# Emitting the four query tiles of the input projection inside the preparation of the recurrent heads, with a z buffer of their own

## The chip, the cores and the metric

The kernel runs on one core of a Trainium2 chip. The metric is the device time of one execution in microseconds (us). A core has five engines that run side by side, each with its own queue of instructions: TensorE (PE in the profile, matrix products), VectorE (DVE), ScalarE (ACT), GpSimd (POOL) and SyncE (SP, which only issues transfers here). An engine takes its queue in order, and an instruction starts when what it depends on is there.

## The reference, cut to what matters

One step of a decoder layer with two kinds of heads, for 512 prompt rows and 8 x 4 sample rows. Everything is fp32.

```python
xp = ffn_half(xp, ffn1_norm, ffn1_wg, ffn1_wu, ffn1_wd)         # the same for the sample rows xs
zp = rms_norm(xp, mix_norm) @ w_in                              # one projection, columns split among the heads
qp, kvp, gp = nsa_heads(zp[..., :NSA_COLS])                     # 512 query, 6 x 128 key/value, 24 gate columns
o_nsa = nsa_prompt(qp, kvp, gp, cmp_w, rel_bias_table)          # compressed, selected and window attention
o_rw, wkv, shift = rwkv_mix(zp[..., NSA_COLS:], ...)            # RWKV-7: token shift, decay, delta rule
xp = xp + concat([o_nsa, o_rw]) @ w_out
xp = ffn_half(xp, ffn2_norm, ffn2_wg, ffn2_wu, ffn2_wd)
y  = rms_norm(xp, final_norm)
```

In `nsa_prompt` the compressed branch takes a softmax of queries times block summaries of the keys (at most 8 blocks); the summed probabilities also choose the blocks of the selected branch.

## The kernel before, in words

The stages follow one another: first feed-forward half, input projection with recurrent heads and attention, output projection, second half. Activations lie as columns, 128 features by 2 x 272 rows (16 sample rows and 256 prompt rows in each half, `SW` to `HW`). A large product is split into a high and a low part of each operand and summed from three products, so one column tile of the input projection (`win_tile`, L385, 8 blocks of the contraction) is 48 matmuls of 128x128 by 128x272 on L155, and its weights are loaded by SyncE (`wraw`, L144) and split by ScalarE (`wh`, L146) and VectorE (`wl`, L148).

There are 25 column tiles. `rwkv_prep` (L511) takes tiles 0 to 13 for the recurrent heads: it loops over two pairs of heads per call and is called twice (head pairs 0 and 1, then 2 and 3). Per pair it forms rates, decays and normalised keys on ScalarE and VectorE (L545 to L574) and multiplies them into blocks (L581). `rwkv_inverse` (L615) inverts the block triangles with a ladder of 30 dependent VectorE instructions between two transposes (L619 to L641). `rwkv_chain` (L681) runs the recurrence, `rwkv_sample` (L761) the sample rows.

`nsa_in` (L407) takes tiles 14 to 24, one for i = 0 to 10: i = 0 to 3 are the queries, 4 and 5 the keys and values for compression, 6 and 8 keys (selected, window), 7 and 9 their values, 10 the gates. It multiplies the sums by the norm `r` into a tile `z`, and stores that to memory through ScalarE's queue (`zq` for queries, `out_kv` for the rest). Values are transposed on TensorE (L434) into `vr`; keys are split into `kk` by four ScalarE copies (L445) and four VectorE differences (L446); i = 8 also writes `out_owk`. The order of the eleven is `ZORD = (0, 1, 2, 3, 4, 5, 10, 7, 9, 6, 8)`.

Queries are read back from `zq`: by `prompt_cmp` as `zr`, four loads of one query tile each through two buffers (L1256), for the scores of the compressed branch (L1258), their softmax (L1259 to L1273), a transpose (L1276) and its copy `PcmT` (L1277); and by the attention as `qd`.

Tiles come from pools. A pool's tag has a fixed number of buffers used in turn: `z` has the tag `xr` of the pool `rot`, two buffers, which the block operands `bk` of the preparation and all z tiles share. PSUM holds two sums of dense tiles (`acc`). The order on each engine is not that of the code: a scheduler reorders instructions when the kernel is built, mostly by the order in which the code emits them and by when their inputs and buffers are thought ready. On the chip each engine then runs its queue strictly in that order. Cache gathers (`kv`, L997) and small loads (`gsum`, L1017) stand in SyncE's queue; the tags of some `kv` buffers are those of the projection's activations (`hh`, `hl`), so they are free when the last dense matmul has read these.

Of the kernel before, what the change touches and what calls it, by code (L numbers as in the profile page):

```python
# [7 lines left out]
F32 = mybir.dt.float32  # L8
# [15 lines left out]
ZORD = (0, 1, 2, 3, 4, 5, 10, 7, 9, 6, 8)  # L24
# [3 lines left out]
HW = 272  # L28
# [19 lines left out]
class Step:  # L48
# [44 lines left out]
    def v(self, i):  # L93
        return self.vec[:, i:i + 1]
# [243 lines left out]
    def mix(self):  # L338
        nc = self.nc
        r = self.norm_end()  # L340
        with ExitStack() as st:
            self.mc = self.pool("mc", 1, st)
            self.un = self.pool("un", 1, st)
            self.orw = self.mc.tile([128, 4, 2, HW], F32, name="orw")
            un1 = self.un1 = self.pool("u1", 1, st)
            with ExitStack() as s0:
                un0 = self.pool("u0", 1, s0, side="right")
                with ExitStack() as s2:
                    self.rwkv_setup(s2)
                    self.lanes = "p"  # L350
                    S0 = self.rwkv_prep(0, r, un0)
                    self.lanes = "q"
                    self.rwkv_inverse(S0[0])
                    self.lanes = "p"
                    S1 = self.rwkv_prep(1, r, un1)
                    nc.scalar.dma_start(self.O["sh"], self.sho.rearrange("p a b -> p (a b)"))
                self.lanes = "q"
                self.ch = self.pool("ch", 1, s0, side="right")
                self.rwkv_chain(0, un0, *S0)
                self.rwkv_inverse(S1[0])  # L360
            self.az = self.pool("az", 1, st, side="right")
            with ExitStack() as s3:
                self.lanes = "p"
                yo = self.rwkv_sample(self.pool("rs", 1, s3, side="right"))
                self.lanes = "q"
                self.ch = self.pool("ch1", 1, s3, side="right")
                self.rwkv_chain(1, un1, *S1)
            self.rwkv_sample_out(yo)
            self.un1 = un1
            self.lanes = "p"  # L370
            self.at = self.pool("at", 1, st, side="right")
            for i in ZORD[0:4]:
                self.nsa_in(i, r)
            self.nsa_open()
            for i in ZORD[4:7]:
                self.nsa_in(i, r)
            cmp = self.prompt_cmp(*self.prompt_blocks())
            for i in ZORD[7:]:
                self.nsa_in(i, r)
            self.attention_setup()  # L380
            bias = self.prompt_bias()
            self.attention(bias, cmp)
            self.w_out()
# [23 lines left out]
    def nsa_in(self, i, r):  # L407
        nc, O = self.nc, self.O
        p = self.win_tile(14 + i)
        if i == 10:  # L410
            nc.vector.tensor_mul(self.gT[:24], p[:24, :, :HW], r[:24])
            nc.scalar.activation(self.gT[:24], self.gT[:24], AF.Sigmoid)
            return
        z = self.rot.tile([128, 2, HW], F32, name="z", tag="xr")
        zt = z[:, :, SW:HW]
        if i < 4:
            nc.vector.scalar_tensor_tensor(z, p[:, :, :HW], 0.125, r, op0=OP.mult, op1=OP.mult)
            nc.scalar.dma_start(self.zq[:, i], z)
            return
        nc.vector.tensor_mul(z, p[:, :, :HW], r)  # L420
        nc.scalar.dma_start(O["kv"][i - 4], z)
        if i < 6:
            for g in range(2):
                for ch in range(2):
                    nc.scalar.activation(self.px[ch * 64:ch * 64 + 64, i - 4, g],
                                         zt[g * 64:g * 64 + 64].rearrange("p h (b c j) -> p h b c j", b=4, c=2)[:, :, :, ch], AF.Copy)
            return
        nc.gpsimd.tensor_copy(self.new[:, i - 6].rearrange("p (h t) -> p h t", h=2), z[:, :, 0:SW])
        b = i // 2 - 3
        if i % 2:  # L430
            p = self.ps()
            for j in range(4):
                c0 = SW + (j % 2) * 128
                nc.tensor.transpose(p[:, j * 128:j * 128 + 128], z[:, j // 2, c0:c0 + 128], self.ident)  # L434
            nc.scalar.activation(self.vr[:, b], p.rearrange("p (j g d) -> p j g d", j=4, g=2), AF.Copy)
            return
        if i == 8:
            for h in range(2):
                nc.scalar.dma_start(O["owk"][4 * h:4 * h + 4, :, 508:512].rearrange("n p t -> p n t"),
                                    z[:, h, 0:SW].rearrange("p (n t) -> p n t", t=4))  # L440
        v = lambda x: x.rearrange("p (h t) -> p h t", h=2)
        for g in range(2):
            for x in range(2):
                zg, k2 = zt[g * 64:g * 64 + 64], self.kk[b][x * 64:x * 64 + 64, g]
                nc.scalar.activation(v(k2[:, 0]), zg, AF.Copy)  # L445
                nc.vector.tensor_sub(v(k2[:, 1]), zg, v(k2[:, 0]).bitcast(F32))  # L446
# [64 lines left out]
    def rwkv_prep(self, si, r, up):  # L511
# [20 lines left out]
        for pi in range(2):  # L532
            p = 2 * si + pi
# [76 lines left out]
            nc.vector.tensor_mul(self.gbs[:, 1, p], samp(pb[0]), samp(v))  # L610
            nc.vector.tensor_mul(c64(self.orw[:, p, 0, SW:HW]), half(pb[0][:, ZS:ZP[0][1]]), half(v[:, ZS:ZP[0][1]]))
            nc.vector.tensor_mul(c64(self.orw[:, p, 1, SW:HW]), half(pb[1][:, :ZW - ZP[1][0]]), half(v[:, ZP[1][0]:ZW]))
        return L, BK, UV, ar, pcp

    def rwkv_inverse(self, L):  # L615
# [979 lines left out]
```

## Time and profile before

| | before |
|---|---|
| time, three runs, us | 1405.24, 1395.78, 1404.97 |
| median, us | 1404.97 |
| profiled execution: time / span, us | 1392.31 / 1390.5 |
| mean granted TensorE clock | 0.974 |
| TensorE busy | 1315.2 us, 95% |
| VectorE, ScalarE, GpSimd busy | 51%, 37%, 19% |
| mixing stage up to the last projection tile | about 500 to 784 us |
| attention | about 784 to 928 us |

The profile is of one execution. Its times are microseconds from the first instruction. A row names an engine, a source line, an operation, out<-in by the program's tile names, partitions and shape; PE is TensorE's multiplying and PEld its loading of weights. [...] An idle time in brackets stands just ahead of the instruction, with what ended it; a transfer's row on a queue is the time of its issue, not of its flight.

### The profile page before, as it was taken

How to read it: one execution, taken by the hardware profiler on the slowest of the kernel's cores; microseconds unless marked ns; L12 is line 12 of the kernel's file. 1: busy time of each engine (PE TensorE's matmuls, PEld its weight loads, DVE VectorE, ACT ScalarE, POOL GpSimd, SP SyncE). 2: the span in 40 equal slices, each digit the busy share in tenths (PEclk: the TensorE clock that was granted, in tenths of full speed). 3: DMA queues.
4: the chain of work that ended last, by engine and by line, in shares of the span. 5: the costliest groups of instructions: out<-in, count | busy, mean ns of one | idle time of the engine just before them, and what ended most of it. 6: DMA issues, size and time to landing. Idle time of an engine off the chain costs nothing.

```text
span 1390.5 us, 31672 instructions
## 1 busy us (share of the span) xinstructions
PE 1315.2 (95%) x13313; PEld 1240.6 (89%) x13313; DVE 706.4 (51%) x1357; ACT 512.7 (37%) x925; POOL 258.9 (19%) x317
## 2 busy tenths in 40 slices
PE   6999999999999998998999779989999999999996
PEld 6999999999999977787678667769999999999996
DVE  6443343333333558869685675765544444442224
ACT  5232232233222555451223455754433333332231
POOL 2073567530000111210003214301000000000000
PEclk9999999999999999699999889999999999999998
DMA  4464465544443311112225528625322222233332
GB/s 157 162 197 121 149 201 186 174 132 116 124 118 114 112 54 46 34 41 73 73 78 180 149 72 243 201 79 179 100 92 84 91 86 90 88 100 108 102 105 84
DMA packets 99328, 163.25 MB, mean 117 GB/s; under 512 B 16185, under 2 KB 42881, under 8 KB 98546
## 3 DMA queue, kind: packets, MB, share of 16 engines
q1 hardware_dynamic: 74258, 114.71, 26.8%
q0 software_dynamic: 9040, 25.24, 6.1%
q10 hardware_dynamic: 15888, 21.28, 5.0%
q8 instruction: 105, 1.72, 0.5%
q14 instruction: 37, 0.30, 0.1%
HBM read 150.19 MB, written 16.72 MB: 120 GB/s over the span
## 4 chain that ended last, share of the span: by engine, by line
PE 68%; DVE 6%; ACT 3%; DMA 3%; issue 2%; POOL 0%; SPq 0%; ACTq 0%; DVEq 0%; POOLq 0%
PE acc L155 53%; PE pp L949 1%; PE pq L952 1%; PE po L949 1%; PE pS L949 1%; DMA kv<-in_slc 1%; PE pq L697 1%; PE pp L480 1%; PE pp L581 1%; DMA kv<-in_slc,idx 1%; DVE ivt L636 1%; PE pq L155 1%; PE pq L722 1%; PE pp L859 0%; DMA kv<-in_wkv 0%
## 5 line engine op out<-in xcount | busy, mean ns | idle before, releaser
L155 PE MATMUL acc<-hl,wh 128*128 128x272 f32 x2064 | 427.4, 292 | 3.9 <-ACT wh L146 3.9
L146 ACT ACTIVATE wh<-wraw 128x512 fp32r<-128x512 f32 x338 | 209.7, 621 | 581.9 <-PE acc L155 537.2
L155 PE MATMUL acc<-hh,wh 128*128 128x272 f32 x1808 | 384.1, 293 | 9.1 <-ACT hh L104 9.1
L148 DVE TENSOR_TENSOR wl<-wraw,wh 128x512 fp32r<-128x512 f32 x338 | 232.0, 687 | 306.2 <-ACT wh L146 304.3
L155 PE MATMUL acc<-hh,wl 128*128 128x272 f32 x1808 | 381.3, 292 | 1.6 <-DVE wl L148 1.6
L155 PEld LDWEIGHTS acc<-hl,wh 128*128 128x128 f32 x2064 | 325.3, 191 | 9.4 <-ACT wh L146 4.2
L155 PEld LDWEIGHTS acc<-hh,wh 128*128 128x128 f32 x1808 | 288.1, 190 | 14.5 <-ACT hh L104 9.1
L155 PEld LDWEIGHTS acc<-hh,wl 128*128 128x128 f32 x1808 | 285.5, 190 | 4.4 <-DVE wl L148 1.9
L903 POOL DMA_INDIRECT cp<-in_cmp,idx x128 | 131.1, 1024 | 98.6 <-issue 37.2
L122 POOL TENSOR_TENSOR ss<-ss,sq 128x544 f32<-128x544 f32 x23 | 31.6, 1374 | 612.4 <-ACT sq L118 597.0
L155 PE MATMUL acc<-ah,wh 128*128 128x272 f32 x660 | 136.9, 289 | 0.0
L155 PE MATMUL acc<-al,wh 128*128 128x272 f32 x660 | 136.3, 288 | 0.0
L155 PE MATMUL acc<-ah,wl 128*128 128x272 f32 x660 | 135.6, 286 | 0.0
L155 PEld LDWEIGHTS acc<-al,wh 128*128 128x128 f32 x660 | 104.0, 188 | 0.0
L155 PEld LDWEIGHTS acc<-ah,wl 128*128 128x128 f32 x660 | 103.3, 188 | 0.0
L155 PEld LDWEIGHTS acc<-ah,wh 128*128 128x128 f32 x660 | 103.0, 188 | 0.0
L190 DVE TENSOR_TENSOR u<-acc,r 128x544 f32<-128x544 f32 x42 | 30.4, 724 | 74.8 <-PE acc L155 74.8
L188 DVE TENSOR_TENSOR t<-acc,r 128x544 f32<-128x544 f32 x42 | 30.4, 724 | 74.1 <-PE acc L155 74.1
L903 POOL DMA_INDIRECT kv<-in_slc,idx x48 | 47.1, 982 | 108.8 <-DVE Y L730 60.3
L193 ACT ACTIVATE ah<-u 128x544 fp32r<-128x544 f32 x44 | 29.0, 658 | 64.1 <-DVE u L191 64.1
L194 DVE TENSOR_TENSOR al<-u,ah 128x544 fp32r<-128x544 f32 x44 | 31.9, 724 | 29.0 <-ACT ah L193 29.0
L1352 ACT ACTIVATE Sp<-Sp,st 128x512 f32<-128x512 f32 (+3 forms) x64 | 35.4, 554 | 9.1 <-DVE st L1350 7.4
(495 smaller groups left out, 1438.8 us busy)
## 6 DMA issues: line engine op xcount, KB each, us to landing
wraw<-in_wg SPq DMA_DIRECT2D x88, 256.0 KB
wraw<-in_wu SPq DMA_DIRECT2D x88, 256.0 KB
wraw<-in_wd SPq DMA_DIRECT2D x80, 256.0 KB
wraw<-in_win SPq DMA_DIRECT2D x50, 256.0 KB
kv<-in_slc SPq DMA_DIRECT2D x80, 128.0 KB
x<-xr ACTq DMA_DIRECT2D x16, 272.0 KB
xr<-x ACTq DMA_DIRECT2D x16, 272.0 KB
kv<-in_wkv SPq DMA_DIRECT2D x8, 512.0 KB
```

What stands on the lines that cost most here:

```text
L122: nc.gpsimd.tensor_add(self.ss, self.ss, sq)
L146: nc.scalar.activation(wh[:, :m], w[:, :m], AF.Copy)
L148: nc.vector.tensor_sub(wl[:, :m], w[:, :m], wh[:, :m].bitcast(F32))
L155: self.nc.tensor.matmul(p[h] if isinstance(p, list) else p[:, h, :HW], a, b[:, h], start=f, stop=l)
L188: nc.vector.tensor_mul(t, pt, r)
L190: nc.vector.tensor_mul(u, pu, r)
L193: nc.scalar.activation(ah[:, f], u, AF.Copy)
L194: nc.vector.tensor_sub(al[:, f], u, ah[:, f].bitcast(F32))
L480: self.nc.tensor.matmul(p[h][:, :b - a], lhsT, rhs[:, a:b], start=True, stop=True)
L903: self.nc.gpsimd.indirect_dma_start(out=tile[:, k], out_offset=None, in_=rows, in_offset=bass.IndirectOffsetOnAxis(ap=self.idx[:, k0 + k:k ...
L949: self.tc.keep_in_program_order(self.nc.tensor.matmul(*args, **kw))
L1352: nc.scalar.activation(S[g][:, :N], S[g][:, :N], AF.Exp, bias=st[:, g:g + 1], scale=-1.0, accum_out=st[:, 2 + g:3 + g])
```

## The change

The four query tiles are no longer emitted ahead of `nsa_open`; each pair of heads in `rwkv_prep` emits one of them at the end of its loop. Their `z` gets a tile `zz` from the pool of the preparation, one buffer, freed with that pool. Lines from L374 to L610 of before are two less after, those from L611 on one less.

```diff
--- before.py
+++ after.py
@@ -369,8 +369,6 @@
             self.un1 = un1
             self.lanes = "p"
             self.at = self.pool("at", 1, st, side="right")
-            for i in ZORD[0:4]:
-                self.nsa_in(i, r)
             self.nsa_open()
             for i in ZORD[4:7]:
                 self.nsa_in(i, r)
@@ -411,7 +409,7 @@
             nc.vector.tensor_mul(self.gT[:24], p[:24, :, :HW], r[:24])
             nc.scalar.activation(self.gT[:24], self.gT[:24], AF.Sigmoid)
             return
-        z = self.rot.tile([128, 2, HW], F32, name="z", tag="xr")
+        z = self.tp.tile([128, 2, HW], F32, name="zz") if i < 4 else self.rot.tile([128, 2, HW], F32, name="z", tag="xr")
         zt = z[:, :, SW:HW]
         if i < 4:
             nc.vector.scalar_tensor_tensor(z, p[:, :, :HW], 0.125, r, op0=OP.mult, op1=OP.mult)
@@ -610,6 +608,7 @@
             nc.vector.tensor_mul(self.gbs[:, 1, p], samp(pb[0]), samp(v))
             nc.vector.tensor_mul(c64(self.orw[:, p, 0, SW:HW]), half(pb[0][:, ZS:ZP[0][1]]), half(v[:, ZS:ZP[0][1]]))
             nc.vector.tensor_mul(c64(self.orw[:, p, 1, SW:HW]), half(pb[1][:, :ZW - ZP[1][0]]), half(v[:, ZP[1][0]:ZW]))
+            self.nsa_in(p, r)
         return L, BK, UV, ar, pcp
 
     def rwkv_inverse(self, L):
```

What the scheduler makes of it is shown at three places.

VectorE, in the preparation of head pair 2, around the end of the ladder of the first inverse (`ivt`, `ivN`). Before:

```order
L637 TENSOR_REDUCE ivN<-ivt 128x2x14
L557 SCALAR_TENSOR_TENSOR sig<-xs_k,vec,sig 128x560
L636 TENSOR_TENSOR ivt<-ivN,ivA 128x450
L560 TENSOR_TENSOR xs_k<-xs_k,sq_6205 128x560
L637 TENSOR_REDUCE ivN<-ivt 128x2x15
L561 TENSOR_TENSOR a<-sig,a 128x560
L639 STREAM_TRANSPOSE ivDt<-ivN 128x32x32
L641 STREAM_TRANSPOSE ivDn<-ivN 128x32x32
L570 TENSOR_TENSOR bk_6447<-a,sq_6205 128x512
L571 TENSOR_TENSOR bk_6448<-xs_k,sq_6205 128x512
```

After:

```order
L638 STREAM_TRANSPOSE ivDt<-ivN 128x32x32
L640 STREAM_TRANSPOSE ivDn<-ivN 128x32x32
L551 TENSOR_SCALAR sig<-pp 128x300
L551 TENSOR_SCALAR sig<-pp 128x260
L148 TENSOR_TENSOR wl<-wraw,wh 128x512
L659 TENSOR_TENSOR ivDt<-pq,ivDt 32x16x16 x2
L555 SCALAR_TENSOR_TENSOR sig<-xs_k,vec,sig 128x560
L558 TENSOR_TENSOR xs_k<-xs_k,sq_6333 128x560
L559 TENSOR_TENSOR a<-sig,a 128x560
L415 SCALAR_TENSOR_TENSOR zz<-acc,r 128x544
L568 TENSOR_TENSOR bk_6575<-a,sq_6333 128x512
L569 TENSOR_TENSOR bk_6576<-xs_k,sq_6333 128x512
```

The products that form `sig`, `xs_k` and `a` of pair 2 stood inside the ladder and ahead of its transposes; they now stand behind both transposes, and the query product `zz` stands between them and the block operands `bk`.

TensorE, at the end of the projection: dense matmuls (L155, `acc`), scores of the compressed branch, transposes of its probabilities (`Pm`) and of the values (`z`). Lines of "..." leave out dense matmuls only. Before, with 20 dense matmuls left out behind the second row, then 6, 51, 6 and 64:

```order
L1258 MATMUL pp<-kcd,zr 128x16 x8
L480 MATMUL pq<-sg,g_5019 128x260
...
L1258 MATMUL pp<-kcd,zr 128x16 x4
...
L1258 MATMUL pp<-kcd,zr 128x16 x4
...
L1276 MATMUL pp<-ident,Pm 64x128 x4
L434 MATMUL pp<-ident,z 128x128 x4
...
L434 MATMUL pp<-ident,z 128x128 x4
...
L883 MATMUL pp<-hid,w_8816 128x512
```

After, with 3 left out and then 13:

```order
L1257 MATMUL pp<-kcd,zr 128x16 x8
...
L1236 MATMUL pp<-w_8816,hx 64x64
...
L1257 MATMUL pp<-kcd,zr 128x16 x8
L1275 MATMUL pp<-ident,Pm 64x128 x4
L432 MATMUL pp<-ident,z 128x128 x8
L882 MATMUL pp<-hid,w_8816 128x512
```

The second half of the scores and all the transposes now stand behind the last dense matmul of the projection.

VectorE at the same place: the end of the softmax (`Pm`, `cmx`), the copy `PcmT`, query splits (`qs`) and the products `z` of the tiles i = 6 and 8. Before:

```order
L1273 TENSOR_TENSOR Pm<-Pm,cmx 128x256
L148 TENSOR_TENSOR wl<-wraw,wh 128x512 x2
L1277 COPY PcmT<-pp 64x512
L420 TENSOR_TENSOR z<-acc,r 128x544
L1329 SCALAR_TENSOR_TENSOR qs<-qd,qs 64x512
L446 TENSOR_TENSOR kk<-z,kk 64x512 x4
L1329 SCALAR_TENSOR_TENSOR qs<-qd,qs 64x512
L420 TENSOR_TENSOR z<-acc,r 128x544
L886 COPY kccT<-pp 64x256 x2
```

After:

```order
L1272 TENSOR_TENSOR Pm<-Pm,cmx 128x256
L1276 COPY PcmT<-pp 64x512
L1328 SCALAR_TENSOR_TENSOR qs<-qd,qs 64x512
L418 TENSOR_TENSOR z<-acc,r 128x544 x2
L1328 SCALAR_TENSOR_TENSOR qs<-qd,qs 64x512
L885 COPY kccT<-pp 64x256
L444 TENSOR_TENSOR kk<-z,kk 64x512 x4
L885 COPY kccT<-pp 64x256
```

In both orders the products stand behind the copy; the two are now next to each other, and no weight split stands between them and the softmax.

## Rows read from the trace of the kernel before

**Rows 1.** Page: the span, and TensorE's busy time, share and instructions.

```profile
span 1390.5 us, 31672 instructions
PE 1315.2 (95%) x13313; PEld 1240.6 (89%) x13313; DVE 706.4 (51%) x1357; ACT 512.7 (37%) x925; POOL 258.9 (19%) x317
```

**Rows 2.** Stretches: length; busy PE, PEld, DVE, ACT, POOL; granted clock; DMA share; GB/s.

```profile
500.00:784.00 284.00, 263.99 (x4156) 223.15 (x4155) 204.29 (x381) 106.64 (x180) 40.32 (x83) 0.96 0.24 76
500.00:540.00 40.00, 34.57 (x400) 30.60 (x400) 25.94 (x47) 20.72 (x35) 9.62 (x25) 1.00 0.14 45
540.00:571.00 31.00, 28.41 (x262) 24.46 (x254) 29.80 (x57) 16.09 (x25) 2.94 (x14) 0.89 0.14 47
571.00:599.00 28.00, 25.91 (x671) 23.01 (x673) 16.40 (x28) 10.36 (x20) 7.72 (x13) 0.70 0.11 34
599.00:629.00 30.00, 26.46 (x394) 22.69 (x393) 22.03 (x34) 15.53 (x24) 4.04 (x10) 1.00 0.14 46
```

**Rows 3.** Timeline, TensorE, preparation: start, length, what [idle before <-releaser].

```profile
536.13 1.10 PE L581 MATMUL pp<-ar,bk 64*64 64x128 f32 x32 [1.91 <-DVE ar L574]
...
556.04 1.04 PE L546 MATMUL pp<-xs_wa,w2a 64*128 64x260 f32 x2 [1.61 <-ACT a L548]
...
571.09 1.26 PE L647 MATMUL pq<-ivDt,L 16*32 16x16 f32 x128 [1.08 <-DVE ivDt L639]
...
604.36 0.60 PE L480 MATMUL pp<-sq,blk 128*128 128x260 f32 x2
...
615.28 1.10 PE L581 MATMUL pp<-ar,bk 64*64 64x128 f32 x32 [1.22 <-DVE ar L574]
```

**Rows 4.** Timeline, VectorE, ladder of the first inverse and pair 2's products.

```profile
542.59 1.98 DVE L619 STREAM_TRANSPOSE ivA<-L 128x1024 f32<-128x1024 f32 x1
...
565.42 0.80 DVE L557 SCALAR_TENSOR_TENSOR sig<-xs_k,vec,sig 128x560 f32<-128x560 f32 x1 [0.55 <-ACT sig L555]
...
568.22 0.75 DVE L561 TENSOR_TENSOR a<-sig,a 128x560 f32<-128x560 f32 x1
568.86 2.17 DVE L639 STREAM_TRANSPOSE ivDt<-ivN 128x1024 f32<-128x1024 f32 x1
```

**Rows 5.** Chain that ended last, in order of time: start, length, what.

```profile
775.85 8.03 PE acc L155 x64
```

**Rows 6.** Timeline, TensorE, end of the projection and first gsum product.

```profile
764.54 0.96 PE L1258 MATMUL pp<-kcd,zr 128*128 128x16 f32 x8
...
773.47 0.60 PE L1276 MATMUL pp<-ident,Pm 128*64 128x128 f32 x4
...
775.20 0.66 PE L434 MATMUL pp<-ident,z 128*128 128x128 f32 x4
...
798.43 0.52 PE L949 MATMUL pp<-Pc,gsum 128*128 128x64 f32 x2
```

**Rows 7.** Timeline, VectorE, softmax of the compressed scores to tile 8's product.

```profile
767.18 0.42 DVE L1259 TENSOR_TENSOR Pm<-pp,cb 128x256 f32<-128x256 f32 x1 [2.54 <-PE pp L1258]
...
772.33 0.42 DVE L1273 TENSOR_TENSOR Pm<-Pm,cmx 128x256 f32<-128x256 f32 x1
...
774.49 0.68 DVE L1277 COPY PcmT<-pp 64x512 f32<-64x512 f32 x1
...
783.96 0.72 DVE L420 TENSOR_TENSOR z<-acc,r 128x544 f32<-128x544 f32 x1 [0.75 <-issue]
```

**Rows 8.** Timeline, ScalarE, the copies of tile 8's keys.

```profile
789.78 2.59 ACT L445 ACTIVATE kk<-z 64x512 fp32r<-64x512 f32 x4 [7.43 <-DMA out_owk<-z]
```

**Rows 9.** Timeline, SyncE's queue: start and length of the issues.

```profile
760.80 1.27 SPq L1256 DMA_DIRECT2D zr<-zq  x2
...
766.06 0.43 SPq L1017 DMA_DIRECT2D gsum<-in_gsum  x1
...
783.90 2.82 SPq L997 DMA_DIRECT2D kv<-in_slc  x5
786.82 5.62 SPq L898 DMA_DIRECT2D out_owv<-vn  x8
```

## The prediction

> **What bounds the kernel now.** I read the page first, then busy time by stretch, then what each engine did and waited for in the two places that the change touches. TensorE is busy 95% of the span [rows 1], so time can only be won where it waits or runs slowly, and lost where it has to wait anew. From the start of the mixing stage to the end of the last win tile (500 to 784 us) it is busy 263.99 of 284 us: 20.0 us idle, spread out [rows 2]. One dense matmul there costs 8.03 / 64 = 0.1255 us [rows 5], so a win tile (48 of them) costs 6.0 us. Two stretches differ. In 540 to 571 us VectorE is busy 29.80 of 31 us and sets the pace, and in 571 to 599 us the granted clock is 0.70 against 1.00 behind it, which alone costs 28 x 0.30 = 8.4 us of capacity [rows 2]. In the preparation TensorE's waits are short and for VectorE or ScalarE: 1.91 us (pair 1's block products), 1.61 (the rate projection of pair 2), 1.08 (the inverse), 1.22 (pair 3) [rows 3]. The last win tile ends at 775.85 + 8.03 = 783.88 us [rows 5]; I call this moment T. Behind it attention is a chain through all engines.
>
> **The change, part by part.** No arithmetic is added: the four query tiles (4 x 48 matmuls, a VectorE product and a store each) run earlier, so whatever dense work they take from the end of the stage is missing there. The order of the changed program shows how much: of the dense work behind the first compressed-score matmul, 20 + 6 + 51 + 6 + 64 = 147 matmuls before, 16 are left.
>
> *The own buffer.* It only takes the query tiles out of the rotation of two that all z tiles shared. No row shows a query tile late for it; I cost it at 0, and its gain is bounded by the idle time there.
>
> *Moved ahead of or behind T.* Before, 16 score matmuls (two groups of 0.96 us as at 764.54), four transposes (0.60), and two groups of value transposes (0.66, and one of the size of the 0.60) ran ahead of T [rows 6]. They now stand behind the last dense matmul. T comes 1.92 + 0.60 + 1.26 = **3.8 us earlier**, and that work returns in the tail, counted below.
>
> *In the preparation.* The tiles are filler between preparation steps, but the scheduler moves other work too. Pair 1: 79 instead of 75 matmuls stand ahead of its block products, so the wait of 1.91 shrinks by 4 x 0.1255 = 0.5. Inverse of heads 0: three VectorE products of pair 2 (0.80, 0.75, 0.75, the first and last are [rows 4]) that stood inside the ladder of 542.59 to 571.03 now follow it, so the ladder ends 2.3 us earlier, while 12 fewer matmuls (1.5 us) stand ahead of it: 0.8 won. But pair 2's products wait for those three: 1.5 lost (0 to 2). Pair 3: from its sum matmul's end (604.36 + 0.60) to its block products (615.28) are 10.3 us [rows 3], which 54 dense matmuls (6.8 us) and the inverse's matmuls (about 2.1 us) fill before; now 43 fill it (5.4 us), so the wait of 1.22 grows by about 1.5. All later steps of chains and inverse 1 have as much filler as before or lack a little, 0 to 1 us. Sum: -0.5 - 0.8 + 1.5 + 1.5 + (0 to 1), hence **+1.7 to +2.2; I take +1.7**. The bounds are -3 (each of the four waits of [rows 3] half filled) and +6 (each of the four grown by 1.5). That the clock changes is a rival below.
>
> *The tail.* Here is the largest term. In the new order VectorE does the products of tiles 6 and 8 (the last two) only behind the softmax of the compressed scores and its copy: their z buffers are the two that tiles 7 and 9 hold until their value transposes, and these stand on TensorE behind the transposes of that softmax. Counted from T:
> the first half of the score matmuls ends 16 x 0.1255 = 2.0 us ahead of T and frees the last query slice's buffer; from the issue of such a load to the use of it were 764.54 - 760.80 = 3.7 us [rows 6, 9], so the last four score matmuls run at T + 1.7 to T + 2.65;
> the softmax took 772.33 + 0.42 - 767.18 = 5.6 us [rows 7] with three weight splits inside it, without them 4.3; I take 5.0;
> transposes 0.60 [rows 6], their copy 0.68, one product of queries of the same size about 0.7, two z products of 0.72 [rows 7].
> That ends at T + 2.65 + 5.0 + 0.6 + 0.7 + 0.7 + 1.4 = T + 11.1. Before, tile 8's z ended at 783.96 + 0.72 = T + 0.8 [rows 7]: **+10.3 us** for everything that hangs on it. On top, the copies of tile 6's keys (four, 2.59 us on ScalarE [rows 8]) lay under dense work and now stand ahead of tile 8's; about 1.9 of them are not covered. Tail: **+12 us**, bounds 8 (softmax 4.3, the key copies hidden, the load 1.5 us faster) and 15 (softmax 5.6, all 2.6 us of key copies, 2 us at the lower clock). The price is paid whole only because attention hung on tile 8's z already: its keys' copies [rows 8] start once the queue behind that z is through.
>
> *The queue past which loads move.* The load of the summing matrix gsum was issued at 766.06, long before the end; now SyncE issues it behind four groups of cache gathers (the first after T took 2.82 us) and eight stores of 5.62 us in sum [rows 9]. 4 x 2.82 + 5.62 plus waits of about 5 us gives T + 22, landing some 3.7 us later, T + 25.7. It is first used at 798.43 = T + 14.6 [rows 6], which the tail pushes to T + 26.6. So I cost it at **0**, covered by the very delay above; without that cover it is up to 11 us late, and if the gathers wait longer, 4 to 5 us.
>
> **Sum:** -3.8 + 1.7 + 12 = +9.9, so **about +10 us**. The profiled execution took 1392.3 (span 1390.5 [rows 1]), 12.7 below the median of the three timed runs, 1404.97; the four lie between 1392.3 and 1405.2. Against the profile the forecast is 1402, against the median 1415. I start from the mean of the middle two, 1400.4: **1410 us**.
>
> **Rivals.** *B, the clock.* [...] With more filler in the preparation it may stay up: -8.4, in all +1.5, **1402**. [...] Against it: the filler ahead of inverse 0 shrinks by 12 matmuls, it does not grow.
> [...]
> *C, more slow stretches.* Behind the shorter filler of pair 3 and of inverse 1 the clock falls once more as in 571 to 599: +8.4, **1418**. Against it: 599 to 629 us, with 3.5 us idle, ran at 1.00 [rows 2].
> *D, faster.* The moved tiles fill waits, and the tail does not grow, because at run time the last score matmuls and their softmax lie under the last tiles. Idle in 500 to 629 us are 5.43 + 2.59 + 2.09 + 3.54 = 13.65 us [rows 2]; with three quarters of it filled (-10) and T's -3.8 returned as tail work, **1390**. It decides if the last query slices land 8 us or more ahead of T; the new order leaves 2 us.
> *E, gsum late* by 4 to 5 us with the forecast's tail: **1415**.
>
> **How the numbers follow.** Forecast (+4 to +14, 1404 to 1414) 0.55; B 0.15; E 0.12; C 0.10; D 0.08. The likeliest is 1410. The range runs from 1395 (B with the tail's lower bound is 1398, and the timed runs differ by up to 3 from their middle) to 1424 (E with the preparation's upper bound, 1415 + 4, and the same 5 us of scatter on top); it leaves out D and what is beyond C. One per cent, 14 us, is about what a measurement of this kernel can tell from no change. From the median that is below 1391 or above 1419. Faster: three quarters of D, 0.06. Slower: half of C, a third of E and an eighth of the forecast, 0.05 + 0.04 + 0.08 = 0.17, and 0.04 for a higher start, 0.21. Same: 0.73.
>
> **What would show it.** Right: the last dense matmul of the projection 2 to 4 us nearer to the start of mixing, VectorE's products of tiles 6 and 8 some 10 us behind it, and the first gsum product near T + 26. Wrong: those two products within 3 us of T (then D); granted clock 1.00 all through 571 to 599 (B); a second stretch near 0.70 (C); the gsum product waiting for its load (E). What would break the working most: a time behind T that attention absorbs in its own waits for cache loads, since then the tail's 12 us would shrink.

## The result and the profile after

The changed kernel takes **1418.6 us** (median of four executions, 1414.35 to 1421.14) against 1400.4 before (four, 1392.25 to 1405.24): 1.0138 times as long, with a 95% interval of 1.0097 to 1.018. A second measurement, of ten executions against 25 of before, gave 1416.2 against 1399.5, a ratio of 1.0113 (1.0072 to 1.0154). So it is 17 to 18 us slower. The forecast was 1410 us, 10 us slower, in a range of 1395 to 1424; the sign and the range held, the size was short by 7 to 8 us. Four of the kernels below (`own_z`, `heads23_only`, `heads01_only`, `dup_tile`) ran at a time in which the kernel before took 1540.0 us too, for a reason that no run shows, so every ratio is to runs of before from the same time.

The profiled executions differ by 22.1 us. The page of after, its span and busy times [rows 1]:

```profile
span 1412.6 us, 31684 instructions
PE 1330.8 (94%) x13313; PEld 1250.3 (89%) x13313; DVE 706.1 (50%) x1357; ACT 513.0 (36%) x925; POOL 255.8 (18%) x317
```

TensorE has the same 13313 instructions and is busy 15.6 us longer with them, at a mean granted clock of 0.959 against 0.974 (in the profile's unit, a share of full speed); VectorE's and ScalarE's busy times are the same within 0.3 us. The rest of the 22.1 us is time in which TensorE stands idle. The end of the projection in TensorE's timeline of after, without most of the dense matmuls; it answers to [rows 6]:

```profile
770.76 1.58 PE L1217 MATMUL pp<-px,w1r 128*64 128x16 f32 x32 [3.14 <-DMA w1r<-in_cw]
...
786.10 1.85 PE L1257 MATMUL pp<-kcd,zr 128*128 128x16 f32 x16
...
790.09 0.41 PE L155 MATMUL acc<-hh,wl 128*128 128x272 f32 x2
790.34 2.04 PE L1257 MATMUL pp<-kcd,zr 128*128 128x16 f32 x16
799.57 1.03 PE L1275 MATMUL pp<-ident,Pm 128*64 128x128 f32 x4 [7.19 <-DVE Pm L1272]
800.39 2.10 PE L432 MATMUL pp<-ident,z 128*128 128x128 f32 x8
...
819.52 0.41 PE L948 MATMUL pp<-Pc,gsum 128*128 128x64 f32 x2 [0.73 <-PE pS L948]
```

The last dense matmul ends at 790.5 us (T; 783.9 before). Behind it run the scores' second half, until T + 1.9, and then TensorE stands idle for 7.19 us until the softmax of the compressed scores is done; before, the same transposes ran 10.4 us ahead of T. Now VectorE in the same place, answering to [rows 7]:

```profile
792.41 0.42 DVE L1258 TENSOR_TENSOR Pm<-pp,cb 128x256 f32<-128x256 f32 x1 [3.01 <-PE pp L1257]
...
797.66 0.69 DVE L1328 SCALAR_TENSOR_TENSOR qs<-qd,qs 64x512 fp32r<-64x512 f32 x1 [1.99 <-ACT qs L1327]
...
798.99 0.43 DVE L1272 TENSOR_TENSOR Pm<-Pm,cmx 128x256 f32<-128x256 f32 x1
800.63 0.68 DVE L1276 COPY PcmT<-pp 64x512 f32<-64x512 f32 x1 [1.22 <-PE pp L1275]
801.35 0.69 DVE L1328 SCALAR_TENSOR_TENSOR qs<-qd,qs 64x512 fp32r<-64x512 f32 x1
802.07 1.36 DVE L418 TENSOR_TENSOR z<-acc,r 128x544 f32<-128x544 f32 x2
...
804.79 0.69 DVE L1328 SCALAR_TENSOR_TENSOR qs<-qd,qs 64x512 fp32r<-64x512 f32 x1 [1.36 <-ACT qs L1327]
```

The products of tiles 6 and 8 end at 803.43 = T + 12.9, where tile 8's ended at T + 0.8 before: they stand in VectorE's queue behind the softmax, as the order said. One thing is new to the forecast: a query split `qs` (the row at 797.66) stands inside the softmax and holds it for 1.99 us, because its load is late. ScalarE's timeline of after (ACTq rows are issues of transfers):

```profile
791.33 1.93 ACTq L1321 DMA_DIRECT2D qd<-zq  x3
793.29 1.28 ACT L1266 ACT_TABLE_LOAD   x1 [6.29 <-PE pp L1257]
794.59 0.42 ACT L1266 ACTIVATE Pm<-Pm 128x256 f32<-128x256 f32 x1
797.00 0.63 ACT L1327 ACTIVATE qs<-qd 128x512 fp32r<-128x512 f32 x1 [1.99 <-DMA qd<-zq]
797.01 2.56 ACTq L1321 DMA_DIRECT2D qd<-zq  x3
```

`qd` and the query tiles `zr` of the compressed scores share two buffers (tag `sq`). While the scores' second half stands behind T, the buffers are held past T: the first `qd` is issued at 791.33 and used at 797.00, and the next is issued only then. SyncE's queue, answering to [rows 9]:

```profile
765.67 2.53 SPq L1214 DMA_DIRECT2D w1r<-in_cw  x4
...
787.09 1.27 SPq L1255 DMA_DIRECT2D zr<-zq  x2
788.55 19.71 SPq L996 DMA_DIRECT2D kv<-in_slc  x20
...
813.63 0.43 SPq L1016 DMA_DIRECT2D gsum<-in_gsum  x1
```

`gsum` is issued at T + 23.1, and the profile puts the 0.73 us that its product at 819.52 waits down to scores (pS), not to it. From T to the first selection score S on VectorE are 52.8 us (843.26), before 39.7 (823.61); from T to the first matmul of the output projection 158.5 us (949.05), before 144.2 (928.05). So 14.3 of the 22.1 us lie behind T, 6.6 ahead of it, and the last 1.1 behind the start of the output projection.

### The profile page after: what moved, and what is told of

It reads as the page before. It is cut to its first block, busy times and chain, and to the rows that moved or that the text cites. A ratio compares the mean times of both kernels' runs of the same rounds, so it can differ in the third digit from the quotient of the medians.

```text
span 1412.6 us, 31684 instructions
## 1 busy us (share of the span) xinstructions
PE 1330.8 (94%) x13313; PEld 1250.3 (89%) x13313; DVE 706.1 (50%) x1357; ACT 513.0 (36%) x925; POOL 255.8 (18%) x317
## 3 DMA queue, kind: packets, MB, share of 16 engines
q1 hardware_dynamic: 74258, 114.71, 26.6%
## 4 chain that ended last, share of the span: by engine, by line
PE 68%; DVE 7%; DMA 3%; ACT 2%; issue 2%; POOL 0%; SPq 0%; DVEq 0%; ACTq 0%
PE acc L155 53%; PE pp L948 2%; PE po L948 1%; PE pq L951 1%; PE pS L948 1%; PE pq L696 1%; DMA kv<-in_slc,idx 1%; DMA qd<-zq 1%; DVE ivt L635 1%; PE pp L778 1%; PE pq L155 1%; PE pp L478 1%; PE pp L579 0%; PE pq L721 0%; PE pp L155 0%
## 5 line engine op out<-in xcount | busy, mean ns | idle before, releaser
L155 PE MATMUL acc<-hl,wh 128*128 128x272 f32 x2064 | 428.5, 293 | 3.9 <-ACT wh L146 3.9
L155 PE MATMUL acc<-hh,wh 128*128 128x272 f32 x1808 | 387.4, 294 | 8.9 <-ACT hh L104 8.9
L155 PE MATMUL acc<-hh,wl 128*128 128x272 f32 x1808 | 384.2, 293 | 1.6 <-DVE wl L148 1.6
L155 PEld LDWEIGHTS acc<-hl,wh 128*128 128x128 f32 x2064 | 327.1, 192 | 6.6 <-ACT wh L146 4.2
L155 PEld LDWEIGHTS acc<-hh,wh 128*128 128x128 f32 x1808 | 290.0, 191 | 15.3 <-ACT hh L104 8.9
L155 PEld LDWEIGHTS acc<-hh,wl 128*128 128x128 f32 x1808 | 287.4, 191 | 4.9 <-DVE wl L148 1.8
L155 PE MATMUL acc<-ah,wh 128*128 128x272 f32 x660 | 136.9, 289 | 0.0
L155 PE MATMUL acc<-al,wh 128*128 128x272 f32 x660 | 136.3, 287 | 0.0
L155 PE MATMUL acc<-ah,wl 128*128 128x272 f32 x660 | 135.6, 286 | 0.0
L155 PEld LDWEIGHTS acc<-al,wh 128*128 128x128 f32 x660 | 104.0, 188 | 0.0
L155 PEld LDWEIGHTS acc<-ah,wl 128*128 128x128 f32 x660 | 103.3, 188 | 0.0
L155 PEld LDWEIGHTS acc<-ah,wh 128*128 128x128 f32 x660 | 103.0, 188 | 0.0
L1351 ACT ACTIVATE Sp<-Sp,st 128x512 f32<-128x512 f32 (+3 forms) x64 | 35.4, 555 | 10.8 <-DVE st L1349 9.1
```

Source lines behind the costliest of these rows:

```text
L155: self.nc.tensor.matmul(p[h] if isinstance(p, list) else p[:, h, :HW], a, b[:, h], start=f, stop=l)
L1351: nc.scalar.activation(S[g][:, :N], S[g][:, :N], AF.Exp, bias=st[:, g:g + 1], scale=-1.0, accum_out=st[:, 2 + g:3 + g])
```

## The experiments

All times are medians. This table gathers all runs; T is the end of the last dense projection matmul, z the end of the last product of tiles 6 and 8, S the first selection score (VectorE), all from timelines.

| kernel | ratio to before (95%) | z - T, us | S - T, us |
|---|---|---|---|
| before / `control_before` | 1 | 0.8 / 0.8 | 39.7 / 39.8 |
| changed / `control_after` | 1.0138 / 1.0113 (1.0072 to 1.0154) | 12.9 / 13.2 | 52.8 / 54.2 |
| `shared_z` | 1.0101 (1.0052 to 1.015) | 13.8 | 53.1 |
| `own_z` | 1.0106 (1.0059 to 1.0153) | 0.8 | 48.8 |
| `own_z_zr` | 1.0059 (1.0025 to 1.0093) | 0.8 | 41.6 |
| `w1_early` | 1.0025 (0.9986 to 1.0063) | 4.8 | 43.6 |
| `own_z_zr_w1` | 0.9997 (0.9959 to 1.0034) | 5.7 | 42.1 |
| `heads23_only` | 1.0035 (1.0007 to 1.0063) | 0.8 | 38.9 |
| `heads01_only` | 1.0022 (0.9978 to 1.0065) | 3.8 | 41.7 |
| `dup_tile` | 1.0123 (1.0075 to 1.0171) | 6.0 | 44.8 |
| `before_w1_early` | 0.9973 (0.9944 to 1.0002) | 0.8 | 38.2 |
| `heads01_w1` | 0.9977 (0.9946 to 1.0008) | 1.7 | 36.5 |

The theories after the first comparison: **tail** (work stranded behind T costs 13 to 14 us), and **preparation** (lower clock and a late weight load ahead of T cost the rest, or most).

**Own z buffers** (`own_z`), buffers of the finished inverse instead of the two of the rotation:

```diff
-        z = ... if i < 4 else self.rot.tile([128, 2, HW], F32, name="z", tag="xr")
+        z = ... if i < 4 else self.un.tile([128, 2, HW], F32, name="zk", tag={6: "iN", 8: "iD"}[i]) if i in (6, 8) \
+            else self.rot.tile([128, 2, HW], F32, name="z", tag="xr")
```

> The changed kernel, but the z tiles of the two key tiles (6 and 8) get buffers of their own instead of the two of the rotation, so their products no longer wait behind the softmax. Theory 'tail' (the products of tiles 6 and 8 behind the softmax cost about 13 us of the 18 to 22): the two products end within 1.5 us of the last dense matmul, the first scores of the attention then wait for the query splits alone, and the time falls by 7 to 10 us below the changed kernel. Rival 'preparation' (the loss lies ahead of the last dense matmul, in slow clock and a late load, and attention would absorb the tail): within 3 us of the changed kernel.

Measured 1554.5 against 1540.0 us, a ratio of 1.0106, hardly below the changed kernel's 1.0113 to 1.0138; the 7 to 10 us expected by the tail theory did not show, though with four executions (1.0059 to 1.0153) the time alone does not rule out 7. The products did move:

```profile
912.60 0.72 DVE L418 TENSOR_TENSOR zk<-acc,r 128x544 f32<-128x544 f32 x1 [2.25 <-PE acc L155]
...
923.32 0.69 DVE L1328 SCALAR_TENSOR_TENSOR qs<-qd,qs 64x512 fp32r<-64x512 f32 x1 [0.93 <-ACT qs L1327]
...
929.63 0.69 DVE L1328 SCALAR_TENSOR_TENSOR qs<-qd,qs 64x512 fp32r<-64x512 f32 x1 [1.62 <-ACT qs L1327]
```

The product of tile 8 starts at T + 0.1, and still query splits come as late as T + 10.8 and T + 17.1 (T is 912.5): the other buffer wait takes the place of the one removed, and S moves by 4 us only.

**Half of the move** (`heads23_only`, `heads01_only`): the tiles of two pairs stay at the old place.

```diff
-            self.nsa_in(p, r)
+            if p in [2, 3]:                      # [0, 1] in heads01_only
+                self.nsa_in(p, r)
+            for i in [0, 1]:                     # ahead of nsa_open; [2, 3] in heads01_only
+                self.nsa_in(i, r)
```

> Only query tiles 2 and 3 are emitted in the preparation (of pairs 2 and 3); 0 and 1 stay at the old place. In the order 102 dense matmuls lie behind the first compressed score (147 before, 16 after) and the softmax's transposes stand 37 ahead of the last. Theory 'tail': the tail is as before, so at most the preparation's share remains, +2 to +5 us over before. Rival 'cost by the number of moved tiles': half of the change's loss, +9 to +10.

> Only query tiles 0 and 1 are emitted in the preparation (of pairs 0 and 1); 2 and 3 stay at the old place. In the order 54 dense matmuls lie behind the first score, but the softmax's transposes and the value transposes stand behind the last dense one, as in the changed kernel. Theory 'tail': +6 to +9 us over before, most of it behind the last dense matmul. Rival 'cost by the number of moved tiles': the same as the other half, +9 to +10; rival 'preparation': what the wait for the late weight load and the slow clock cost, with two dense tiles kept for later both go, so +0 to +3.

Measured +0.35% (5.4 us) and +0.22% (3.4 us). The first has no tail (S at T + 38.9); its loss, a little above the 2 to 5 expected, must lie elsewhere, and no run shows where. The second has a small tail (z at T + 3.8, S 2 us later than before), and less loss than the 6 to 9 that the tail theory expected: it is nearer to the 0 to 3 of its rival. By the medians neither costs half of the change, and both together cost 8.8 us where the four tiles cost 17; but both intervals reach up to 9 or 10 us. S is clearer: it is no later than before in the one and 2 us later in the other, where the four tiles cost 13. The tail is not one per moved tile, it sets in when the last of the filler behind the scores goes.

**A dense tile more** (`dup_tile`): the first query tile's sum is computed again at the old place and not used.

```diff
+            p = self.win_tile(14)
+            zd = self.rot.tile([128, 2, HW], F32, name="zd", tag="xr")
+            nc.vector.tensor_copy(zd, p[:, :, :HW])
             self.nsa_open()
```

> The changed kernel with the first query tile computed a second time, without use, at the old place: 48 dense matmuls (6.0 us) more, of which 36 come behind the first compressed score. Theory 'clock' (the sparse stretch behind inverse 1 runs at the lower level because its dense filler is gone, costing about 8 us, and the late weight load costs 2 to 3): the added tile gives that back, so the time is within 3 us of the changed kernel and the granted clock of that stretch is 0.95 or more. Rival 'clock and filler don't matter': 6 us slower than the changed kernel.

Measured 1558.9 us, a ratio of 1.0123, that of the changed kernel: 6.0 us of added matmuls cost nothing that four executions can tell (1.0075 to 1.0171). The clock theory named that number, but for the wrong reason: its profile shows the lower clock that it should have removed (0.50 in 821 to 831 us, 0.64 in 831 to 841 us). What it did was to shorten the tail by 8 us (S at T + 44.8).

**The two kernels again** (`control_before`, `control_after`):

> The kernel before, unchanged, profiled on the chip of this call. Theory 'the clock falls in a stretch because of the change': no second stretch of lower clock about 190 to 220 us behind pair 0's block products, and the last dense projection matmul 281 us (280 to 283) behind them. Rival 'a fall in that stretch comes and goes from run to run': such a stretch here too, and 288 to 291 us.

> The changed kernel, unchanged, on the chip of this call. Expected the ratio of the first measurement, 1.010 to 1.018, the last dense matmul 289 to 291 us behind pair 0's block products, the products of tiles 6 and 8 ending 13 us behind it. If the loss depended on the chip, a ratio within 1.005.

The ratio came again (1.0113), and so did the distance from T to the output projection: 163.2 us against 148.7, 14.5 more. The stretch of low clock that the first profile of the changed kernel has in 700 to 720 us did not come again. Here are stretches (columns of [rows 2]) of before, `control_before`, the changed kernel and `control_after`, in this order, each from its own profile:

```profile
755.00:783.90 28.90, 28.90 (x249) 27.29 (x245) 16.72 (x34) 10.12 (x19) 3.60 (x5) 1.00 0.41 119
```

```profile
757.00:780.00 23.00, 23.00 (x209) 20.13 (x208) 6.73 (x15) 3.65 (x9) 6.39 (x8) 0.64 0.33 96
```

```profile
700.00:720.00 20.00, 19.21 (x207) 9.58 (x202) 9.24 (x15) 3.92 (x8) 0.00 (x0) 0.59 0.01 2
```

```profile
700.00:720.00 20.00, 18.83 (x437) 12.21 (x428) 14.60 (x31) 6.24 (x12) 0.00 (x0) 1.00 0.02 4
```

The kernel before ran at 1.00 in one profile and at 0.64 in the other, 8.3 us lost in 23 (length times the missing share of the clock); the changed kernel at 0.59 in one (8.2 us lost) and at 1.00 in the other. In `control_before` T lies at 799.3, 15.4 us later than in the first profile of the same kernel, and 298 us behind pair 0's block products, which neither theory had named. Its time, 1411.9, is just above the 25 other executions of before, which spread from 1390.9 to 1408.7 us with mean granted clocks of 0.975 to 0.961.

Here is all of the stretch from pair 0's block products to T, for the same four in the same order and then for `own_z_zr` and `own_z_zr_w1` (both further below). The granted clock is the third number from the end:

```profile
502.60:783.87 281.27, 262.96 (x4148) 222.34 (x4148) 201.82 (x376) 106.07 (x178) 37.65 (x76) 0.96 0.24 76
500.92:799.27 298.35, 281.16 (x4148) 235.18 (x4148) 200.71 (x376) 106.19 (x178) 39.47 (x76) 0.89 0.23 72
500.37:790.50 290.13, 270.43 (x4121) 226.23 (x4121) 193.80 (x359) 99.30 (x168) 35.94 (x76) 0.92 0.22 68
502.75:792.17 289.42, 268.75 (x4121) 227.95 (x4121) 193.71 (x359) 99.27 (x168) 35.89 (x76) 0.92 0.21 68
500.54:796.27 295.73, 276.66 (x4134) 231.99 (x4134) 198.67 (x367) 102.80 (x174) 36.81 (x78) 0.90 0.23 72
500.25:780.50 280.25, 262.93 (x4100) 223.21 (x4102) 195.71 (x366) 105.25 (x174) 36.82 (x77) 0.94 0.24 75
```

Length times clock is 270, 266, 267, 266, 266 and 263 us. Ahead of T the two kernels differ by less than two profiles of the kernel before, and what makes a profile long there is the granted clock.

**Early compression weights** (`w1_early`): their buffers no longer lie in the attention's pool, whose memory is free only when chain 1 is done.

```diff
-            w1 = c.tile([128, 2, 8, 64], F32, name="w1r", tag="kv", bufs=KVB)
+            w1 = self.un.tile([128, 2, 8, 64], F32, name="w1r", tag=("iA", "iN", "iD", "iA")[j0 // 8])
```

> The changed kernel, but the four tiles of compression weights (w1r) get the buffers of the inverse instead of those of the attention's pool, so their loads no longer wait for the end of chain 1. In the order 133 dense matmuls instead of 43 then lie behind the first product with them and 57 instead of 16 behind the first score. Theory 'late load': the wait of 3.1 us and the lower clock behind it go and the first scores run under dense work, together 8 to 12 us below the changed kernel. Rival 'only the wait': 2 to 3 us below it. Rival 'tail by the z buffers alone': within 1 us ahead of the last dense matmul, and the tail as long as before the edit.

Measured 1402.9 us, 13.3 below `control_after`, a little more than the 8 to 12 expected. SyncE's queue shows three of the four loads 66 us earlier than in the changed kernel:

```profile
700.02 11.45 SPq L1214 DMA_DIRECT2D w1r<-in_cw  x3
...
746.70 0.57 SPq L1214 DMA_DIRECT2D w1r<-in_cw  x1
```

With them the scores run under dense work, and S comes 43.6 us behind T. The rival of 2 to 3 us falls: the wait itself (3.03 us in `control_after`) is the smaller part of what the late load does in this order.

**Own buffers for z and the query loads** (`own_z_zr`), the four `zr` in the finished inverse's two tiles, so that `qd` has the `sq` buffers to itself:

```diff
-            zr = self.rot.tile([128, 2, PW], F32, name="zr", tag="sq")
+            if r % 2 == 0:
+                z2 = self.un.tile([128, 2, 2, PW], F32, name="zr", tag=("iA", "iN")[r // 2])
+            zr = z2[:, r % 2]
+            # z of tile 6: self.un, tag "iD"; z of tile 8: self.rot, tag "ss", bufs=1
```

> The changed kernel with own buffers for the z tiles of 6 and 8 and for the four query loads zr, so that neither products nor query splits (qd, which shared its two buffers with zr) wait behind the compressed scores. Theory 'tail is made of buffer waits': the first selection score of the attention (S) 42 to 45 us behind the last dense matmul, against 52.8 in the changed kernel and 39.7 before, and 8 to 10 us below the changed kernel. Rival 'the tail is the softmax chain itself': no more won than with own z buffers alone (S 48.8 us behind), 4 us.

Measured 1407.2 us, 9.1 below `control_after`, and S at T + 41.6, as the tail theory had it. TensorE still waits 8.39 us for the softmax, and the attention's scores stand behind its transposes, but then their queries and keys are ready: they begin at T + 14.1 instead of T + 19.2 (809.74 in after), without the waits that follow there:

```profile
804.66 1.03 PE L1277 MATMUL pp<-ident,Pm 128*64 128x128 f32 x4 [8.39 <-DVE Pm L1274]
...
810.35 1.20 PE L948 MATMUL pS<-kk,qs 128*128 128x512 f32 x4
```

**Shared z** (`shared_z`), the other half of the change undone: `z = self.rot.tile(..., tag="xr")` for the query tiles too.

> The changed kernel without the own buffer: the query tiles stay in the preparation, but their z takes the two rotating buffers that the block operands and the other z tiles share. The order at the end of the projection is the same (15 dense matmuls behind the first score, none behind the second half). Theory 'the own buffer is free and needless' (no query tile waited for its buffer): within 4 us of the changed kernel, so 13 to 20 us over before. Rival 'the own buffer keeps the preparation from waiting': the block operands of the next pair wait for the store of a query tile, 5 us or more slower than the changed kernel.

Measured 1415.0 us, a ratio of 1.0101 (1.0052 to 1.015), within 2 us of `control_after`: the own buffer does nothing that can be told.

**Both edits** (`own_z_zr` and `w1_early` together):

> Both earlier edits together on the changed kernel: own buffers for the z tiles of 6 and 8 and for the query loads, and early compression weights. Theory 'the loss is the tail, and the wait for the weight load' (both edits take the same tail away once): the whole loss goes, within 4 us of before. Rival 'the two gains add' (9 and 13 us): 5 us or more below before, since the moved tiles then fill waits.

Measured 1396.8 against 1398.7 us: the whole loss is gone, and the 5 us below before that the rival named did not show. Whether the two gains add is not shown: by the ratios they are 7.6 and 12.3 us, and 16.2 together, a difference within the intervals. The tail is no shorter with both edits than with `own_z_zr` alone (S at T + 42.1 and 41.6; output projection at T + 149.5 and 149.1), yet the ratio falls from 1.0059 to 0.9997, by 8.7 us. So the early weights gain something besides the tail. In the profiles it lies ahead of T: 295.73 against 280.25 us in the rows above, nearly all of it clock. That the early weights raise the clock in other executions too is not shown.

**Early weights on the kernel before**, and **half of the move with early weights**:

> The kernel before with the early compression weights alone. The wait at their first product was 0.83 us in its profile and 147 dense matmuls lie behind the first score in either order, so theory 'the late load hurts only where the filler is gone' gives -1 us, -3 to +1. Rival 'the early load removes falls of the clock in any order': 5 us or more below before.

> Query tiles 0 and 1 in the preparation, 2 and 3 at the old place, and early compression weights. In the order 99 dense matmuls lie behind the first score, the softmax's transposes stand 31 ahead of the last dense one and the value transposes 27, so the products of tiles 6 and 8 need not wait. Theory 'tail': no tail is left, and with two tiles as filler of the preparation 0 to 4 us below before. Rival 'preparation' (the moved tiles lose 2 us ahead of the last dense matmul whatever follows): 1 to 3 us over before.

Measured 1397.2 and 1396.1 us. Both intervals hold 1, so neither beats the kernel before by more than can be told. `before_w1_early` says little of its theory: three of its loads were not waited for, but the fourth, issued at 747.83, was, by 3.48 us, so in that order the edit did not make all of the load early enough. `heads01_w1` had the shortest tail of all (S at T + 36.5), as the tail theory had it.

## Why the prediction was right, and where it was short

*The tail*, the largest term, was right in kind: +12 forecast, +13.1 at S and +14.3 at the output projection measured. By its parts: the scores ended at T + 1.9 (2.65 forecast; the query loads had come in time), the softmax took 799.42 - 792.41 = 7.0 us (5.0), the transposes 1.03 (0.60; the granted clock in 795 to 800 us was 0.51), and the rest as forecast; the products ended at T + 12.9 (11.1). The 2 us at a lower clock in the upper bound are a guess for which no run shows a figure: in the 26 us behind T the granted clock was 0.59; in the kernel before it was 0.72 in the 26 us from 784 us on. The term that was mis-sized is the softmax. "Three weight splits inside it, without them 4.3; I take 5.0" misread the rows of before: between the softmax's first and last product stand one weight split and one product.

```profile
767.98 0.68 DVE L148 TENSOR_TENSOR wl<-wraw,wh 128x512 fp32r<-128x512 f32 x1
...
770.41 0.72 DVE L420 TENSOR_TENSOR z<-acc,r 128x544 f32<-128x544 f32 x1 [1.20 <-DMA tri<-in_tri]
```

Above all it counted what leaves VectorE's queue and missed what enters it: a query split of 0.69 us that first waits 1.99 us for a load. Without these 2.7 us the softmax took 4.3 us, as forecast. The one query product in the forecast's sum, 0.7 us behind the copy, is another (the row at 801.35). `own_z` shows that the z buffers alone, on which the forecast hung the tail, are not what holds it; `own_z_zr` shows that together with the query loads' buffers they are. The query loads' buffers alone were not tried, so whether the z buffers are needed at all stays open.

*Moved ahead of or behind T* (-3.8) *and the preparation* (+1.7): together -2.1 forecast, with T 2 to 4 us nearer to the start of mixing. The first pair of profiles shows T 6.6 us later, of which 8.2 us are the low clock in 700 to 720 and 3.14 - 0.83 = 2.3 the wait for the compression weights; the second pair, of the same two kernels, shows it 7.1 us earlier. So these two terms can't be checked at their size, and the agreement that either pair would give is luck. In the medians, 17 to 18 us less the tail's 14.3 leave some 3 us ahead of T. By `own_z_zr`, whose tail is nearly gone and which is still 0.59% over before, it would be some 8 us (3.5 to 13). Both are above the forecast, and how much of the loss lies there stays open. The step that looked at too little is "all later steps of chains and inverse 1 have as much filler as before or lack a little, 0 to 1 us": it looked at filler and not at a load. The buffers of these weights lie in memory that chain 1 frees when its last state is stored. In the chain of waits of after:

```profile
761.89 3.59 DMA out_pS<-T
...
765.67 4.84 DMA w1r<-in_cw
```

The store and the load, 8.4 us, are covered by the 35 dense matmuls (4.4 us) that stand there in either order. Before, the store gave way sooner (issued at 738.39, the loads at 740.23) and the wait was 0.83 us; in `control_before` it was 2.22 and in `control_after` 3.03. So the wait was there before, and what the change adds to it is 1 to 2 us. Its removal alone would not explain the 13 us of `w1_early`: S comes 9 to 11 us nearer to T there, since the scores run under dense work. Nor would it explain the 8.7 us that the same edit gains when the tail is gone already; a clock that falls behind the wait would (see the last section), but that is argued and not shown. The single waits of the preparation that the forecast moved are small in both (pair 1's fell from 1.91 to 1.44 us, against 0.5 forecast; pair 3's, forecast to grow by 1.5, went, and the rate projection's grew from 1.61 to 2.54).

*The own buffer* at 0: nothing else can be told (`shared_z`, to some 7 us). *gsum* at 0: right, covered by the tail; issued at T + 23.1 (22 forecast) and used at T + 29.0 (26.6), by the profile it was not waited for. Rival E falls.

*Rival B*, a clock that stays up behind inverse 0: falls. The same stretch after:

```profile
571.00:599.00 28.00, 25.14 (x605) 22.63 (x607) 15.75 (x23) 11.22 (x18) 6.27 (x13) 0.66 0.12 41
```

0.66 against 0.70 [rows 2]: ahead of inverse 0 there were 12 fewer dense matmuls, as the forecast had counted, and the clock was low again. That more filler keeps it up was the author's guess, and no run shows what more filler there would have done. *Rival C*, one more slow stretch, is what the first profile showed, and its 1418 is nearly the measured time; but that profile's stretch ran at 1.00 in `control_after`, and such stretches come and go in both kernels. So C met the time by luck, and no one stretch is shown to be the cause. Whether the change makes them more frequent is open: the changed kernel's ten executions had a mean granted clock of 0.959 against 0.966 in 25 of before, but that mean also holds the tail (0.59 in the 26 us behind T in the first profile). *Rival D* falls: the tail grew.

The start from the mean of the middle two runs was right (1400.4; before is 1399.5 in 25 runs), and it mattered: the profiled run of before was among its fastest. The chance of 0.21 for slower by over 1% was too low by the same missing 7 to 8 us, since the forecast already stood at +0.7%. That the measured time lies in the range is partly luck: it is above the 1404 to 1414 that the prediction gave its own sum, and the upper bound was drawn from a late `gsum` and a slower preparation, not from a softmax that waits for a load. Two slips in the working moved nothing: the preparation's four terms sum to 1.7 to 2.7, not to 2.2, and the four executions differ by up to 8 us from their middle, not by 3.

## What to carry to other kernels

Dense work that is moved forward as filler is taken from somewhere: look at what ran under it there, above all at the last chain of small steps before the next stage, and count that chain from the end of the dense work as a wait. When a chain loses its cover, list every buffer it holds and every load that waits for these buffers; freeing only the first one found moved the wait by 4 of 13 us and the time by nothing that could be told. And take a stretch of low clock for an effect only when a second profile of both kernels shows it.

## What was not expected of the hardware

The granted clock of one and the same kernel differs between executions in whole stretches: 1.00 or 0.64 in one place, 1.00 or 0.59 in another, about 8 us each, where 25 executions spread over 18 us. In each of the eight profiles in which TensorE had waited 2.2 to 3.5 us ahead of a product with the compression weights `w1r`, the granted clock was down there: 0.66 in the 5 us behind the wait of 3.14 us in the changed kernel, 0.64 in 757 to 780 us of `control_before` (2.22 us), 0.66 in 752 to 762 us of `before_w1_early` (3.48 us, inside this stretch), and 0.50 to 0.52 in a stretch of 10 us behind the wait in `control_after`, `own_z`, `own_z_zr`, `dup_tile` and `shared_z`. With a wait of 1.60 us it was 0.50 too (`heads01_only`, 893.8 to 903.8 us), and in the two profiles with 0.67 and 0.83 us (`heads23_only` and before) it was 1.00. Nor is it bound to these products: in `w1_early`, where they had no such wait, TensorE idled 1.77 us in 761.7 to 771.7 us, and the granted clock was 0.92 there and 0.74 in the next 10 us.
